# The gates of a recurrent mixer, two heads on a diagonal or one head to each half of the array's rows

## The chip, the cores and the metric

The kernel runs on one core of one Trainium2 chip. The metric is the device time of one launch in microseconds (us). The kernel before took 1994.26 us, the median of three runs (1993.06 to 1998.03).

## The reference, cut to what matters

One decoder layer over 2048 positions (and 16 learned ones ahead of them) of width 1024. After a norm, one projection feeds three token mixers (pooling, a convolution of 31 taps, and a gated linear recurrence), whose outputs are projected back; a squared-ReLU MLP and a last norm follow. The change is in the recurrent mixer, which has 512 channels in 8 heads of 64:

```python
def _rglru_branch(gate_in, x_in, conv_w, conv_b, w_a, b_a, w_x, b_x, lam):
    xc = _causal_depthwise_conv(x_in, conv_w, conv_b)
    xh = xc.reshape(B_, T, RG_HEADS, RG_HD)
    r = jax.nn.sigmoid((jnp.einsum('bthc,hcd->bthd', xh, w_a).reshape(B_, T, D_RNN) + b_a).astype(f32))
    i = jax.nn.sigmoid((jnp.einsum('bthc,hcd->bthd', xh, w_x).reshape(B_, T, D_RNN) + b_x).astype(f32))
    log_a = -RG_C * r * jax.nn.softplus(-lam.astype(f32))
    a = jnp.exp(log_a)
    mult = jnp.sqrt(-jnp.expm1(2.0 * log_a))
    h = _linear_scan(a, mult * (i * xc.astype(f32)))
    return (jax.nn.gelu(gate_in.astype(f32)) * h).astype(x_in.dtype)
```

Each head of 64 channels is multiplied by its own 64 x 64 matrix twice: by w_a for the gate r and by w_x for the gate i.

## The kernel before, in words

Channels lie on the 128 partitions, positions along the free dimension. The sequence is worked through in four chunks of 512 positions; chunk 0 has the 16 learned positions ahead, 528 in all, and is multiplied in two sub-ranges of 264 (`subs_of`, L364).

Every fp32 product is made of three matmuls: each operand is split into a high part (rounded, on ScalarE, L110) and a low part (the rest, on VectorE, L111), and high x high, high x low and low x high are added up in PSUM (`PRODS`, L270). The large weights come from HBM in tiles of 128 x 512 on SyncE's queue, six loaded ahead (WR) and four split ahead (WH); these splits are given a raised priority (`Weights.split`, L257).

The list `items` (L890) is the order of the large products: W, the input projection (`mm_tile`, L278); O, the output projection (`mm_tile`); U, the up-projection (`up_unit`, `mm_block`, L302, seven products of 256 columns in place of eight); D, the down-projection (`mm_tile` and `mm_pair`, L278 and L292). While TensorE works on these, the mixers, norms and loads of the next stage are generators; after each item `pump` (L866) takes steps from them up to a budget. A `Mix` (L647) has a lane for the taps of each half of the convolution and one for the recurrent calls, the pooling and the GELU gates. The framework then orders each engine's instructions by their place in the program and by when their operands are ready; every engine runs its list in that order.

The recurrent mixer is `gen_rg` (L561), called for i = 0 to 3 in every chunk, 16 calls. One call has two heads, head 2i on partitions 0 to 63 and head 2i + 1 on 64 to 127. It computes the short convolution (L566, L568), splits the result (`split_new`), and multiplies it by the gate weights: for each of the two gates a 128 x 128 block with the two heads' matrices on its diagonal and zeros elsewhere (`_blockdiag`, L1023). Each product is three matmuls by `mm3` (L311 to L313) into a PSUM tile of the pool pb, which has two buffers, and a sigmoid on ScalarE (L579) writes r or g with the bias of the channel. After that come an exponential, a tanh and a square root on ScalarE (L584, L586, L589), products on VectorE (L587 to L596) and the scan (L598). The last calls of a chunk come ahead of the output projection of the chunk, which needs all the mixers' outputs (`need_mix`, L883).

The gate weights, 128 x 1024, are loaded and split once by `load_consts` (L207), in two halves of 512 columns, each through one of the two buffers of xr. The weights that `gen_fold` (L156) multiplies ahead of time (pools, pws, w_fold) come through the same two buffers, behind them. The biases lie in one small tensor, `vecs`, a column for 128 channels (`_VECS`, `vc`).

Of the kernel before, what the change touches and what calls it, by code (L numbers as in the profile page):

```python
# [26 lines left out]
F32R = mybir.dt.float32r  # L27
AF = mybir.ActivationFunctionType
ALU = mybir.AluOpType

P = 128
D = 1024
KB = D // P
# [4 lines left out]
FG = 4  # L38
# [19 lines left out]


_VECS = [  # L60
    ("g1", 8), ("g2", 8), ("gf", 8), ("psc", 2), ("lam", 4), ("ba", 4), ("bx", 4),
    ("rcb", 4), ("cb", 2), ("lng", 2), ("lnb", 2), ("rcw", 16), ("cw", 62),
]
_VOFF = {}
# [15 lines left out]
def build(nc, tc, x0, xr, w_in, w_out, w_fold, w_up, w_down, vecs, gates, pools, pws, out):  # L80
# [18 lines left out]
    def t_(tag, cols, bufs, dt=F32):  # L99
        shape = [P] + (list(cols) if isinstance(cols, (list, tuple)) else [cols])  # L100
        return sb.tile(shape, dt, name=nm(tag), tag=tag, bufs=bufs)
# [4 lines left out]
    def ps_back():  # L106
        return pb.tile([P, NT], F32, name=nm("pb"), tag="pb")

    def split(hi, lo, src):
        A.activation(out=hi, in_=src, func=AF.Copy)  # L110
        V.tensor_tensor(out=lo, in0=src, in1=hi.bitcast(F32), op=ALU.subtract)  # L111
# [5 lines left out]
    def vc(name, i=0):  # L117
        o, _ = _VOFF[name]
        return vec[:, o + i : o + i + 1]
# [18 lines left out]
    def w_raw(src, tag="xr", bufs=2):  # L138
        n = src.shape[-1]
        t = t_(tag, 512, bufs)[:, :n]  # L140
        nc.sync.dma_start(out=t, in_=src)
        return t
# [62 lines left out]
        yield 1400  # L205

    def load_consts():  # L207
        hl = t_("c_gw", (2, 1024), 1, F32R)
        for c0 in (0, 512):
            split(hl[:, 0, c0 : c0 + 512], hl[:, 1, c0 : c0 + 512], w_raw(gates[:, c0 : c0 + 512]))  # L210
        cst["gw"] = hl
        yield 1500

        lam = vr("lam")
        s = t_("sp", (8, 4), 1)
        al, e, den, w, w2, q, m = (s[:, i, :] for i in range(7))
        V.tensor_scalar(out=al, in0=lam, scalar1=-1.0, scalar2=None, op0=ALU.mult)
        V.tensor_scalar(out=m, in0=al, scalar1=0.0, scalar2=None, op0=ALU.max)
        V.tensor_tensor(out=al, in0=al, in1=lam, op=ALU.max)
        A.activation(out=e, in_=al, func=AF.Exp, scale=-1.0)  # L220
        V.tensor_scalar(out=den, in0=e, scalar1=2.0, scalar2=None, op0=ALU.add)
        V.reciprocal(den, den)
        V.tensor_tensor(out=w, in0=e, in1=den, op=ALU.mult)
        V.tensor_tensor(out=w2, in0=w, in1=w, op=ALU.mult)
        NTERM = 10
        V.tensor_scalar(out=q, in0=w2, scalar1=1.0 / (2 * NTERM + 1), scalar2=1.0 / (2 * NTERM - 1), op0=ALU.mult, op1=ALU.add)
        for i in range(NTERM - 2, -1, -1):
            V.tensor_tensor(out=q, in0=q, in1=w2, op=ALU.mult)
            V.tensor_scalar(out=q, in0=q, scalar1=1.0 / (2 * i + 1), scalar2=None, op0=ALU.add)
        V.tensor_tensor(out=q, in0=q, in1=w, op=ALU.mult)  # L230
        V.scalar_tensor_tensor(out=q, in0=q, scalar=2.0, in1=m, op0=ALU.mult, op1=ALU.add)
        csp = t_("csp", (2, 4), 1)
        V.tensor_scalar(out=csp[:, 0, :], in0=q, scalar1=-8.0, scalar2=None, op0=ALU.mult)
        V.tensor_scalar(out=csp[:, 1, :], in0=q, scalar1=4.0, scalar2=None, op0=ALU.mult)
        cst["csp"] = csp
        yield 2500
# [127 lines left out]
    def subs_of(o, full=True):  # L364
        if o.c == 0:
            return [(0, 264), (264, 528)] if full else [(META, W0)]
        return [(0, NT)]
# [193 lines left out]
    def gen_rg(o, i):  # L561
# [9 lines left out]
        w = cst["gw"]  # L571
        r = t_("t", W0, TB)
        g = t_("t", W0, TB)
        for q, (dst, bias) in enumerate(((r, "ba"), (g, "bx"))):
            for s0, s1 in subs_of(o):
                ps = ps_back()
                o_ = q * 512 + i * P
                mm3(ps[:, : s1 - s0], [(w[:, 0, o_ : o_ + P], w[:, 1, o_ : o_ + P], hi[:, s0:s1], lo[:, s0:s1])])
                A.activation(out=dst[:, s0:s1], in_=ps[:, : s1 - s0], func=AF.Sigmoid, bias=vc(bias, i))  # L579
        yield 620  # L580
        csp = cst["csp"]
        a = t_("t", W0, TB)
# [450 lines left out]
def _chan(v):  # L1033
    return np.ascontiguousarray(np.reshape(v, (-1, P)).T)


def _layout(inputs):
# [6 lines left out]
    def wt(w):  # L1044
# [6 lines left out]
    cols = {  # L1051
        "g1": _chan(a["mix_norm_g"][0]), "g2": _chan(a["mlp_norm_g"][0]), "gf": _chan(a["final_norm_g"]),
        "psc": _chan(a["pool_scale"][0]), "lam": _chan(a["rg_lambda"][0]), "ba": _chan(a["rg_b_a"][0]),
        "bx": _chan(a["rg_b_x"][0]), "rcb": _chan(a["rg_conv_b"][0]), "cb": _chan(a["convb_dw_b"][0]),
        "lng": _chan(a["convb_ln_g"][0]), "lnb": _chan(a["convb_ln_b"][0]),
        "rcw": rcw.reshape(4, 4, P).transpose(2, 1, 0).reshape(P, 16),
        "cw": cw.reshape(CONVK, 2, P).transpose(2, 1, 0).reshape(P, 2 * CONVK),
    }
    vecs = np.concatenate([cols[n] for n, _ in _VECS], axis=1)
    gates = np.concatenate([_blockdiag(a["rg_w_a"][0]), _blockdiag(a["rg_w_x"][0])], axis=1).reshape(P, 1024)  # L1060
    pools = _blockdiag(a["pool_w"][0].transpose(0, 2, 1)).reshape(P, 256)
    pws = a["convb_pw_w"][0].T.reshape(2, P, 256).transpose(1, 0, 2).reshape(P, 512)
    w_out = a["w_out"][0]
# [6 lines left out]

_SHAPES = {
    "x0": (KB, P, W0), "xr": (NCH - 1, KB, P, NT), "w_in": (14, P, D), "w_out": (KB, P, 512), "w_fold": (4, P, D), "w_up": (32, P, D),
    "w_down": (FG, KB, P, D), "vecs": (P, NVEC), "gates": (P, 1024), "pools": (P, 256), "pws": (P, 512),
}


# [15 lines left out]
```

## Time and profile before

| | |
|---|---|
| runs before, median (lowest, highest) | 1994.26 us (1993.06, 1998.03) |
| the profiled execution's own time | 1989.49 us |
| its span, first to last instruction | 1987.7 us |
| granted TensorE clock, mean | 0.992 |
| TensorE busy, share of the span | 1927.7 us, 97% |
| TensorE weight loads | 1685.3 us, 85% |
| VectorE busy | 1580.9 us, 80% |
| ScalarE busy | 1127.3 us, 57% |
| HBM over the span | 149 GB/s |

In the profile PE is TensorE's matmuls, PEld its weight loads, DVE VectorE, ACT ScalarE, SPq the queue of SyncE, which issues the loads. L579 is line 579 of the kernel. A row of the timeline has the start in us, the duration, engine, line, operation, the tile written and the one read, the shapes and a count; in brackets stands how long the engine was idle ahead of it and what ended that. A row of a tile or line gives the count and the shortest, median and longest duration in ns. The chain is the work that ended last, followed back from the last instruction: each piece was released by the one ahead of it. Matmuls are pipelined: a record is longer than the step to the next one.

### The profile page before, as it was taken

What the parts mean: (1) busy time and instruction counts of PE and PEld (TensorE: products, weight loads), DVE (VectorE), ACT (ScalarE), POOL (GpSimd) and SP (SyncE); (2) the same over time, 40 slices, a digit from 0 to 9 for tenths busy, and PEclk for the clock granted to TensorE, in tenths of its full rate; (3) what the DMA queues carried; (4) which work ended last, traced back from release to release, by engine and by line L of the source; (5) the groups of instructions that cost most, each with busy time, mean ns of one, the idle gap of its engine ahead of it and who ended that gap; (6) DMA issues with size and microseconds to landing.
All of it is one profiled execution on the core that took longest, in us unless ns stands there. A gap on an engine that the chain in (4) does not pass through costs nothing.

```text
span 1987.7 us, 31314 instructions
## 1 busy us (share of the span) xinstructions
PE 1927.7 (97%) x11220; PEld 1685.3 (85%) x11220; DVE 1580.9 (80%) x2557; ACT 1127.3 (57%) x1907; POOL 0.2 (0%) x4
## 2 busy tenths in 40 slices
PE   8999999999999899999999999999999999999997
PEld 7888787888887689898988878988989889889897
DVE  7988787998979899984777689987668587656477
ACT  6575463636586445683666453675648446355364
POOL 0000000000000000000000000000000000000000
PEclk9999999999999999999999999999999999999999
DMA  6415578748443534353534543534445435545354
GB/s 196 133 53 189 181 254 267 254 124 270 125 130 90 186 100 147 110 161 94 165 113 142 172 135 93 163 106 149 132 127 151 135 102 158 162 143 149 112 175 144
DMA packets 166956, 297.77 MB, mean 150 GB/s; under 512 B 18320, under 2 KB 24592, under 8 KB 166800
## 3 DMA queue, kind: packets, MB, share of 16 engines
q1 hardware_dynamic: 166800, 295.77, 48.6%
q8 instruction: 88, 1.44, 0.3%
q14 instruction: 68, 0.56, 0.1%
HBM read 268.43 MB, written 27.26 MB: 149 GB/s over the span
## 4 chain that ended last, share of the span: by engine, by line
PE 73%; DVE 13%; DMA 5%; issue 4%; ACT 4%; SPq 0%; DVEq 0%; ACTq 0%
PE pm L278 41%; PE pm L302 13%; PE pw L302 11%; PE pm L292 7%; DVE wh L111 3%; DMA xr<-d_xr 2%; DMA s<-d_w_up 1%; DVE ca L534 1%; DVE fr L795 1%; ACT wh L110 1%; DVE t L568 1%; PE pb L311 1%; DVE H L111 0%; DVE h L828 0%; DVE U L804 0%
## 5 line engine op out<-in xcount | busy, mean ns | idle before, releaser
L110 ACT ACTIVATE wh<-wr 128x512 fp32r<-128x512 f32 x876 | 546.0, 627 | 669.7 <-PE pm L278 411.5
L278 PE MATMUL pm<-U,wh 128*128 128x512 f32 (+1 forms) x3504 | 790.2, 384 | 1.4 <-DVE wh L111 1.3
L278 PEld LDWEIGHTS pm<-U,wh 128*128 128x128 f32 x3504 | 634.7, 188 | 143.3 <-DVE wh L111 3.1
L111 DVE TENSOR_TENSOR wh<-wr,wh 128x512 fp32r<-128x512 f32 x876 | 598.5, 687 | 187.2 <-ACT wh L110 181.2
L302 PE MATMUL pm<-H,wh 128*128 128x256 f32 x3072 | 392.7, 283 | 4.7 <-DVE wh L111 2.9
L302 PEld LDWEIGHTS pm<-H,wh 128*128 128x128 f32 x3072 | 378.4, 189 | 9.2 <-DVE wh L111 4.4
L302 PE MATMUL pw<-H,wh 128*128 128x256 f32 x2304 | 301.4, 284 | 16.5 <-DVE fr L795 9.2
L302 PEld LDWEIGHTS pw<-H,wh 128*128 128x128 f32 x2304 | 284.9, 190 | 22.3 <-issue 7.2
L278 PE MATMUL pm<-H,wh 128*128 128x512 f32 (+1 forms) x1344 | 272.9, 361 | 13.5 <-ACT H L390 7.3
L278 PEld LDWEIGHTS pm<-H,wh 128*128 128x128 f32 x1344 | 227.7, 193 | 55.7 <-ACT H L390 7.3
L292 PE MATMUL pm<-U,wh 128*128 128x512 f32 (+1 forms) x768 | 176.5, 388 | 0.0
L292 PEld LDWEIGHTS pm<-U,wh 128*128 128x128 f32 x768 | 140.0, 188 | 30.9
L534 DVE SCALAR_TENSOR_TENSOR ca<-Pbv,vec,ca 128x512 f32<-128x512 f32 x180 | 127.0, 745 | 0.0
L828 DVE TENSOR_TENSOR h<-h,pm 128x512 f32<-128x512 f32 (+1 forms) x106 | 71.2, 674 | 49.7 <-PE pm L278 35.9
L804 DVE TENSOR_TENSOR U<-fr,U 128x512 fp32r<-128x512 f32 x128 | 87.3, 685 | 7.9 <-ACT fr L803 7.8
L801 ACT ACTIVATE fr<-fr 128x512 f32<-128x512 f32 x128 | 79.2, 621 | 25.2 <-DVE fr L820 22.5
L795 DVE TENSOR_TENSOR fr<-pw,fr 128x512 f32<-128x512 f32 x128 | 87.8, 686 | 5.5 <-PE pw L302 3.1
L802 ACT ACTIVATE U<-fr 128x512 fp32r<-128x512 f32 x128 | 79.3, 623 | 1.5
L803 ACT ACTIVATE fr<-fr 128x512 f32<-128x512 f32 x128 | 78.7, 618 | 0.3
L346 DVE TENSOR_TENSOR ss<-ss,fr 128x512 f32<-128x512 f32 (+1 forms) x84 | 54.0, 643 | 19.3 <-ACT fr L345 18.2
L337 DVE RECIPROCAL rs<-rs 128x512 f32<-128x512 f32 (+2 forms) x17 | 53.9, 3168 | 10.6 <-ACT rs L335 10.5
L795 DVE TENSOR_TENSOR fr<-pm,q 128x512 f32<-128x512 f32 x64 | 43.7, 683 | 2.8 <-PE pm L302 2.4
(202 smaller groups left out, 1136.3 us busy)
## 6 DMA issues: line engine op xcount, KB each, us to landing
wr<-d_w_down SPq DMA_DIRECT2D x272, 256.0 KB, 3.0
wr<-sums SPq DMA_DIRECT2D x256, 256.0 KB, 3.3
wr<-d_w_up SPq DMA_DIRECT2D x192, 256.0 KB, 3.0
wr<-d_w_in SPq DMA_DIRECT2D x92, 256.0 KB, 2.9
xr<-d_xr SPq DMA_DIRECT2D x56, 256.0 KB, 3.0
t<-d_w_up SPq DMA_DIRECT2D x32, 256.0 KB, 4.0
wr<-wo_fold SPq DMA_DIRECT2D x32, 256.0 KB, 2.7
wr<-d_w_out SPq DMA_DIRECT2D x32, 256.0 KB, 2.7
```

Of the source, the lines that this page charges most:

```text
L110: A.activation(out=hi, in_=src, func=AF.Copy)
L111: V.tensor_tensor(out=lo, in0=src, in1=hi.bitcast(F32), op=ALU.subtract)
L278: T.matmul(ps[:, : s1 - s0], w[k // 4][:, a, (k % 4) * P : (k % 4 + 1) * P], rhs[k][:, b, s0:s1], start=(k == 0 and j == 0), stop=(k == KB ...
L292: T.matmul(ps[:, : s1 - s0], w[k // 4][:, a, (k % 4) * P : (k % 4 + 1) * P], rhs[k][:, b, s0:s1], start=(k == 0 and j == 0), stop=(k == KB ...
L302: T.matmul(ps, w[:, a, k * P : (k + 1) * P], op[k // 2][:, b, (k % 2) * 256 : (k % 2) * 256 + 256], start=(k == 0 and j == 0), stop=(k == ...
L534: V.scalar_tensor_tensor(out=a, in0=o.ub[i][:, k : k + NT], scalar=vc("cw", i * CONVK + k), in1=a, op0=ALU.mult, op1=ALU.add)
L795: V.tensor_tensor(out=out.rearrange("p (a c) -> p a c", a=2), in0=ps.rearrange("p (a c) -> p a c", a=2), in1=x.unsqueeze(1).broadcast_to([ ...
L801: A.activation(out=r, in_=r, func=AF.Relu)
L802: A.activation(out=f[:, 0], in_=r, func=AF.Square)
L803: A.activation(out=r, in_=r, func=AF.Square)
L804: V.tensor_tensor(out=f[:, 1], in0=r, in1=f[:, 0].bitcast(F32), op=ALU.subtract)
L828: V.tensor_tensor(out=h, in0=h, in1=ps[:, : s1 - s0], op=ALU.add)
```

## The change

The block-diagonal gate weights go. The weight tile has 512 columns in place of 1024: for each call i 128 columns, in which rows 0 to 63 hold [w_a | w_x] of head 2i and rows 64 to 127 hold [w_x | w_a] of head 2i + 1. A matmul uses 64 rows, one head, and gives both gates of that head on the 128 partitions of its result: for the even head r on partitions 0 to 63 and i on 64 to 127 (PSUM tile pa), for the odd head i on 0 to 63 and r on 64 to 127 (pb_). The matmuls of the two heads alternate, each head with its own PSUM tile. Six matmuls for each sub-range stay six. The sigmoids are four in place of two for a sub-range, each of 64 partitions: r of both heads stays on its partitions; i is written to the other half of the partitions, so that it comes to lie with its channel. For that the bias of i is stored with its halves exchanged (`bxs`). `load_consts` has one load and one split in place of two.

```diff
-    ("g1", 8), ("g2", 8), ("gf", 8), ("psc", 2), ("lam", 4), ("ba", 4), ("bx", 4),
+    ("g1", 8), ("g2", 8), ("gf", 8), ("psc", 2), ("lam", 4), ("ba", 4), ("bxs", 4),
...
     def load_consts():
-        hl = t_("c_gw", (2, 1024), 1, F32R)
-        for c0 in (0, 512):
-            split(hl[:, 0, c0 : c0 + 512], hl[:, 1, c0 : c0 + 512], w_raw(gates[:, c0 : c0 + 512]))
+        hl = t_("c_gw", (2, 512), 1, F32R)
+        split(hl[:, 0], hl[:, 1], w_raw(gates))
         cst["gw"] = hl
         yield 1500
...
         r = t_("t", W0, TB)
         g = t_("t", W0, TB)
-        for q, (dst, bias) in enumerate(((r, "ba"), (g, "bx"))):
-            for s0, s1 in subs_of(o):
-                ps = ps_back()
-                o_ = q * 512 + i * P
-                mm3(ps[:, : s1 - s0], [(w[:, 0, o_ : o_ + P], w[:, 1, o_ : o_ + P], hi[:, s0:s1], lo[:, s0:s1])])
-                A.activation(out=dst[:, s0:s1], in_=ps[:, : s1 - s0], func=AF.Sigmoid, bias=vc(bias, i))
+
+        low, high = slice(0, 64), slice(64, P)
+        for s0, s1 in subs_of(o):
+            n = s1 - s0
+            pa, pb_ = ps_back(), ps_back()
+            for j, (a, b) in enumerate(PRODS):
+                for ps, h in ((pa, low), (pb_, high)):
+                    T.matmul(ps[:, :n], w[h, a, i * P : (i + 1) * P], (hi, lo)[b][h, s0:s1], start=(j == 0), stop=(j == 2))
+            for dst, ps, to, of, bias in (
+                (r, pa, low, low, "ba"), (r, pb_, high, high, "ba"), (g, pa, low, high, "bxs"), (g, pb_, high, low, "bxs"),
+            ):
+                A.activation(out=dst[to, s0:s1], in_=ps[of, :n], func=AF.Sigmoid, bias=vc(bias, i)[of])
         yield 620
...
-        "bx": _chan(a["rg_b_x"][0]), "rcb": _chan(a["rg_conv_b"][0]), "cb": _chan(a["convb_dw_b"][0]),
+        "bxs": np.roll(_chan(a["rg_b_x"][0]), 64, axis=0), "rcb": _chan(a["rg_conv_b"][0]), "cb": _chan(a["convb_dw_b"][0]),
...
-    gates = np.concatenate([_blockdiag(a["rg_w_a"][0]), _blockdiag(a["rg_w_x"][0])], axis=1).reshape(P, 1024)
+    gates = np.concatenate([
+        np.concatenate([a["rg_w_a"][0][0::2], a["rg_w_x"][0][0::2]], axis=2),
+        np.concatenate([a["rg_w_x"][0][1::2], a["rg_w_a"][0][1::2]], axis=2),
+    ], axis=1).transpose(1, 0, 2).reshape(P, 512)
```

More of the change, by code (lines that the diff above doesn't have):

```diff
@@ L1072 @@
     "x0": (KB, P, W0), "xr": (NCH - 1, KB, P, NT), "w_in": (14, P, D), "w_out": (KB, P, 512), "w_fold": (4, P, D), "w_up": (32, P, D),
-    "w_down": (FG, KB, P, D), "vecs": (P, NVEC), "gates": (P, 1024), "pools": (P, 256), "pws": (P, 512),
+    "w_down": (FG, KB, P, D), "vecs": (P, NVEC), "gates": (P, 512), "pools": (P, 256), "pws": (P, 512),
 }
```

## The prediction

> **What bounds the kernel now.** I read the page first, then the waits, then the gate matmuls by their tile and in the timeline, then the chain of waits in the stretches where they stand.
>
> ```profile
> PE 1927.7 (97%) x11220; PEld 1685.3 (85%) x11220; DVE 1580.9 (80%) x2557; ACT 1127.3 (57%) x1907; POOL 0.2 (0%) x4
> PE 73%; DVE 13%; DMA 5%; issue 4%; ACT 4%; SPq 0%; DVEq 0%; ACTq 0%
> ...
> ACT wh L110 <- PE pm L278: 411.5, 231, 3.2
> ```
>
> TensorE is busy 97% and holds 73% of the chain that ended last; ScalarE mostly waits for TensorE (411.5 us ahead of the weight split of L110). So TensorE time saved is time saved, except where the chain leaves TensorE. The gates are a small part of TensorE's work:
>
> ```profile
> L311 PE MATMUL pb<-hl,c_gw x40: 279/392/498, 81.2 to 1492.1; 128*128 128x512 f32 x24, 128*128 128x264 f32 x16
> L579 ACT ACTIVATE t<-pb,vec x40: 463/678/691, 82.7 to 1495.4; 128x512 f32<-128x512 f32 x24, 128x264 f32<-128x264 f32 x16
> ...
> 568.19 0.41 PE L311 MATMUL pb<-hl,c_gw 128*128 128x512 f32 x1
> ...
> 569.60 1.08 PE L292 MATMUL pm<-U,wh 128*128 128x512 f32 x4
> ```
>
> L311 has 24 + 16 matmuls, and L312 and L313 follow each of them: 72 of 512 columns (12 calls of the recurrent mixer, six each) and 48 of 264 (4 calls in chunk 0, two sub-ranges each). From 568.19 to 569.60 six of 512 columns take 1.41 us, 0.235 us each from start to start; a record of 512 columns lasts 0.39 us (the median of L311), of which 0.16 us are a tail that the next one covers. With 0.12 us for 264 columns (below), all gate matmuls are 72 x 0.235 + 48 x 0.12 = 23 us, and half of that is the most that the change could save.
>
> Where does the chain leave TensorE near the gates? In chunk 0 it runs on VectorE from 96 to 133 us, and in chunk 1 through ScalarE, up to the output projection at 626.59 us, where TensorE stands idle for 2.93 us:
>
> ```profile
> 95.98 1.25 DVE h L598
> ...
> 132.80 0.65 ACT hl L110
> ...
> 571.65 0.69 ACT t L579
> ...
> 612.97 0.63 ACT t L579 x2
> ...
> 626.59 7.62 PE L278 MATMUL pm<-H,wh 128*128 128x512 f32 x25 [2.93 <-DVE H L111]
> ```
>
> At the gates of chunks 2 and 3, and at the first of chunk 1, it stays on TensorE.
>
> **The change part by part.**
>
> *The matmuls.* Their number (120), columns and weight width stay; each now uses 64 rows, and two that follow one another use different halves, different weights and different PSUM banks. No row shows a matmul of 64 rows. A pair lies between one pitch (0.235 us, full overlap) and two (0.47 us, none). What the two would still share is the weight load, and its rate is bounded by the narrow matmuls:
>
> ```profile
> 97.89 0.39 PE L312 MATMUL pb<-hl,c_gw 128*128 128x264 f32 x1 [0.30 <-DVE st L600]
> 98.11 0.29 PE L313 MATMUL pb<-hl,c_gw 128*128 128x264 f32 x1
> 98.24 0.28 PE L312 MATMUL pb<-hl,c_gw 128*128 128x264 f32 x1
> 98.36 0.28 PE L313 MATMUL pb<-hl,c_gw 128*128 128x264 f32 x1
> ```
>
> From 98.24 to 98.36 is 0.12 us with a load in it, so a load takes at most that. I take the low end: 0.24 us for a pair at 512 columns, two loads, since the halves share neither rows, nor operands' partitions, nor a bank. At 264 columns two loads are as long as two matmuls were: no gain in chunk 0. [...]
>
> A call of 512 columns then starts its matmuls at 0, 0.12, 0.24 ... 0.60 and frees TensorE at 0.60 + 0.235 = 0.835 us: 0.57 us of 1.41 are saved. Where the lo half of the operand comes late, the six are cut in two:
>
> ```profile
> 580.91 0.73 PE L311 MATMUL pb<-hl,c_gw 128*128 128x512 f32 x2 [1.17 <-ACT hl L110]
> ...
> 585.70 0.50 PE L312 MATMUL pb<-hl,c_gw 128*128 128x512 f32 x1
> ```
>
> Pieces of two and four save 0.115 + 0.345 = 0.46. Of the 12 calls nine lie where TensorE holds the chain: the first of chunk 1 and all of chunks 2 and 3, of which the last of each chunk is cut. That is 7 x 0.57 + 2 x 0.46 = **-4.9 us**. The other three of chunk 1 (568, 580 and 604 us, 1.5 us more) only lengthen the idle time at 626.59.
>
> *Changes between 128 and 64 rows.* Each uncut piece has one on either side; today there are none. The floor is nothing, if the next weights are still loaded ahead. The next price is an uncovered load, as after a wait: 97.89 to 98.11 is 0.22 us where 0.12 follows at 98.24, so 0.10 us. The ceiling adds the tail: 0.16 + 0.10 = 0.26 us. I take 0.10, the only one that the kernel's own restarts show. The nine calls make 11 pieces, 22 changes: **+2.2 us**. Of chunk 0 only the first call (81 to 84 us) is on TensorE's chain; three pieces, 6 changes: **+0.6 us**. [...]
>
> *The sigmoids.* 40 become 80, of 64 partitions each. Half the partitions don't shorten VectorE's work in this trace (0.70 and 0.71 us), and I take the same for ScalarE:
>
> ```profile
> 117.13 0.70 DVE L512 TENSOR_TENSOR s<-s 64x525 f32<-64x525 f32 x1
> ...
> 125.14 0.71 DVE L515 TENSOR_TENSOR s<-s 128x525 f32<-128x525 f32 x1
> ...
> 101.41 1.28 ACT L584 ACT_TABLE_LOAD   x1
> ...
> 104.02 1.28 ACT L579 ACT_TABLE_LOAD   x1
> ```
>
> By the median and the minimum of L579, the long and the short ones, ScalarE gains 24 x 0.68 + 16 x 0.46 = 24 us. Behind the added sigmoids queue the weight splits of L110, on which TensorE depends, and the rest of the mixer. In chunks 2 and 3 ScalarE's waits for TensorE (411.5 us in all) and four weight tiles split ahead hide 1.36 us a call: nothing; without that cover 8 x 1.36 = 11 us. In chunk 1 the chain passes the sigmoids twice (571.65 and 612.97), each time with two more of 0.68: **+2.7 us** at 626.59 (between 0, if half the rows are cheaper or other work makes room, and 4.1, if a third call counts). In chunk 0 a call has four more of 0.46, 1.9 us. Against that the exponential now comes ahead of the last sigmoid (101.41), and its table is changed back for that one (104.02); with all products of a sub-range ready together these 1.28 us may go. VectorE has its convolution taps to fill in. Of 0 to 3 x 1.9 = 5.7 us I take **+1.0 us**.
>
> *The two PSUM buffers* of the gates are held until the third and fourth sigmoid, not the first and second. In chunk 0 the second sub-range waits for that, two sigmoids longer, at most 1.0 us in each of 4 calls. TensorE has projection matmuls to put between, as it has now: nothing.
>
> *The constants.* One load of gate weights and one split go.
>
> ```profile
> 42.61 3.85 DMA xr<-d_gates
> ...
> 50.90 3.27 DMA xr<-d_w_fold
> ...
> 47.87 0.33 SPq L141 DMA_DIRECT2D xr<-d_pools  x1
> ...
> 54.97 0.50 PE L311 MATMUL pb<-hl,H 128*128 128x512 f32 x1 [2.04 <-ACT hl L148]
> ```
>
> The chain itself passes here: both gate loads hold both buffers of xr, so pools waits on SyncE's queue until the first split has freed one (47.87), and w_fold until pools is read (50.90). With one load pools goes out at once, some 4 us earlier. TensorE waits for that w_fold for 2.04 us: **-2.0 us** (between -2.04 and 0). Next late is TensorE itself.
>
> Sum: -4.9 + 2.2 + 0.6 + 2.7 + 1.0 - 2.0 = **-0.4 us**. On the profiled execution's own 1989.5 us that is 1989.1. That execution lies 4.8 us under the median of the runs, 1994.3, which I keep as the base: 1993.9 us. About 0.3%, 6 us, is what a measurement of this kernel can tell from no change.
>
> **The rivals.**
>
> *A drain at every change (slower).* Place: both sides of each piece, on TensorE. Some 28 pieces (12 in chunk 0, where the second sub-range would no longer be cut, 16 elsewhere), 56 changes at 0.26 us, all on the path: +14.6 - 6.4 (the savings of all 12 calls) - 2.0 + 3.7 (sigmoids) = +9.9 us, 2004.2. It ends slower from 0.19 us a change on, where 56 x 0.19 passes 6 + 4.7. For it: the tail of 0.16 us is there to be waited for. Against: in chunk 0 VectorE holds the chain, so most of the changes there would be hidden. [...]
>
> *Changes free, sigmoids hidden (faster).* -4.9 - 2.0 = -6.9 us, with the 1.5 us of chunk 1 -8.4: 1985.9 to 1987.4. For it: TensorE's 97% and ScalarE's 43% of idle time. Against: in chunk 1 the chain passes through the sigmoids.
>
> *The halves don't overlap*, so the change doesn't do what its form suggests: 0 saved, +2.2 + 0.6 + 2.7 + 1.0 - 2.0 = +4.5 us, 1998.8; with the drain, 7.3 for 2.8, +9.0, 2003.3. For it: no row shows two matmuls overlap beyond the tail. Against: the halves share nothing that the trace shows but the weight load.
>
> **How the numbers follow.** Forecast 0.45, all of it no change. Free changes 0.24: faster. Drain 0.20: slower. No overlap 0.11: 0.03 no change, 0.08 slower. So faster 0.24, same 0.48, slower 0.28. The range reaches from the fastest case, 1985, to the drain, 2005; what a rearranged order of the engines' lists adds or takes no row prices, and that is the part left out.
>
> **What would show it.** Overlap: six gate matmuls of 512 columns free TensorE after 0.84 us; without overlap after 1.4 or more. Changes: the steps into and out of a piece are longer than the usual pitch by 0.10 (mine), 0.26 (drain) or 0. Sigmoids: 80 of them, 0.68 us each at 512 columns, and an idle time of 2.9 + 2.7 = 5.6 us or more at the output projection of chunk 1. Constants: no wait at the first fold matmul near 55 us. I am wrong if the wait of the fold stays, if the one at 626.59 doesn't grow, or if TensorE gains new waits for split weights in chunks 2 and 3.

## The result and the profile after

| | before | after |
|---|---|---|
| runs, median (lowest, highest) | 1993.33 us (1991.4, 1998.03), 6 runs | 2000.44 us (1997.3, 2002.48), 6 runs |
| the profiled execution's own time | 1989.49 us | 1999.71 us |
| its span | 1987.7 us | 1997.9 us |

Three of the six runs before are those of the prediction. After over before is 1.0031, 95% interval 1.002 to 1.0043: the change makes the kernel slower by 6.2 us (4.0 to 8.6). The prediction was 1993.9 us, no change. The time lies within its range, near that of the drain rival, and, as the experiments show, not for that rival's reason.

The page of the kernel after, engines, chain and the group of the sigmoids:

```profile
PE 1932.1 (97%) x11220; PEld 1678.3 (84%) x11220; DVE 1579.1 (79%) x2556; ACT 1150.1 (58%) x1943; POOL 0.2 (0%) x4
...
PE 71%; DVE 12%; ACT 6%; DMA 5%; issue 5%; SPq 0%; DVEq 0%; ACTq 0%
...
L584 ACT ACTIVATE t<-pb,vec 64x512 f32<-64x512 f32 (+1 forms) x80 | 48.1, 601 | 8.6 <-PE pb L580 7.0
```

The matmuls number as many as before. ScalarE's 80 sigmoids take 48.1 us, and its share of the chain goes from 4% to 6% while TensorE's falls from 73% to 71%: the chain spends less of its time on TensorE.

The timeline of TensorE after, at the second to fourth recurrent call of chunk 1 and at the output projection behind them:

```profile
573.43 1.60 PE L301 MATMUL pw<-H,wh 128*128 128x256 f32 x12
574.96 0.97 PE L580 MATMUL pb<-hl,c_gw 64*128 64x512 f32 x6
575.86 1.89 PE L291 MATMUL pm<-U,wh 128*128 128x512 f32 x7
...
595.61 0.49 PE L580 MATMUL pb<-hl,c_gw 64*128 64x512 f32 x2 [2.29 <-ACT hl L110]
596.03 0.96 PE L277 MATMUL pm<-U,wh 128*128 128x512 f32 x3
...
617.02 0.49 PE L580 MATMUL pb<-hl,c_gw 64*128 64x512 f32 x2
617.45 0.73 PE L277 MATMUL pm<-U,wh 128*128 128x512 f32 x2
...
630.03 0.86 PE L277 MATMUL pm<-H,wh 128*128 128x512 f32 x3
631.95 1.23 PE L277 MATMUL pm<-H,wh 128*128 128x512 f32 x3 [1.06 <-ACT wh L110]
636.49 1.22 PE L277 MATMUL pm<-H,wh 128*128 128x512 f32 x2 [3.31 <-ACT H L110]
640.07 10.31 PE L277 MATMUL pm<-H,wh 128*128 128x512 f32 x34 [2.35 <-DVE H L111]
```

Six gate matmuls now free TensorE after 0.90 us (574.96 to 575.86) in place of 1.41: the halves overlap. But the gates of the third call come 20.65 us behind those of the second (595.61), and before it was 12.7 us (568.19 to 580.91). And the 34 matmuls behind the last wait take 10.31 us, 0.30 each, where 41 took 11.32 us before (0.276) and a step at full clock is 0.235:

```profile
626.59 11.32 PE L278 MATMUL pm<-H,wh 128*128 128x512 f32 x41 [2.93 <-DVE H L111]
```

Both belong to a stretch in which the kernel loses time. The windows view of TensorE alone shows it, from the first to the 480th of the same matmuls (the gates' are not counted). Its columns are the stretch, its length, TensorE's busy time (with the matmuls in it), its granted clock, the DMA share and GB/s. Before:

```profile
574.17:707.45 133.28, 120.97 (x493) 0.96 0.40 125
...
626.80:630.21 3.41, 3.41 (x9) 0.51 0.00 0
```

After:

```profile
580.55:718.72 138.17, 123.17 (x493) 0.93 0.39 120
...
634.64:644.88 10.24, 6.04 (x13) 0.50 0.12 36
```

The stretch grows by 4.9 us: idle time (length less busy time) from 12.3 to 15.0, +2.7, and busy time, +2.2, for the same matmuls and those of the gates. The second rows say why they take longer: at the output projection the granted clock is one half for 3.41 us before and for 10.24 us after, and a step from matmul to matmul is 0.43 us there and 0.23 behind it. Over the whole stretch the trace has half the clock for 10.2 us before and 20.5 us after; of that, TensorE is busy in 8.1 and 13.4 us, and half of it, 4.0 and 6.7 us, is lost: 2.65 us more. Of these, 1.3 are lost at the projection; 1.7 in a window of 3.41 us from 597.03 on, behind the wait of 2.29 us at the third call's gates, which before has no counterpart; and 0.3 less than before is lost further on, at the sums of the norm.

The wait of the fold is smaller, not gone (the waits of TensorE after; before it was 2.04 us):

```profile
PE pb L310 <- ACT hl L148: 1.5, 1, 1.5
```

The two profiled executions differ by 10.2 us, more than the medians, and of the rest little can be credited to the change. The first 1200 matmuls, chunk 0's gates among them, take 248.0 us for 245.7 (245.2 to 251.2 in the kernels run here). Between them and this stretch the profiled executions of all kernels run here take between 324 and 335 us (before 328.5, after 332.6) and lose between 2.9 and 9.2 us to the half clock, in no order that goes with the kernels; behind it after is 1.0 us shorter.

### The profile page after: what moved, and what is told of

It is laid out like the page before. It is cut to its first block, busy times and chain, and to the rows that moved or that the text cites. A ratio compares the mean times of both kernels' runs of the same rounds, so it can differ in the third digit from the quotient of the medians.

```text
span 1997.9 us, 31356 instructions
## 1 busy us (share of the span) xinstructions
PE 1932.1 (97%) x11220; PEld 1678.3 (84%) x11220; DVE 1579.1 (79%) x2556; ACT 1150.1 (58%) x1943; POOL 0.2 (0%) x4
## 3 DMA queue, kind: packets, MB, share of 16 engines
q1 hardware_dynamic: 166656, 295.51, 48.1%
## 4 chain that ended last, share of the span: by engine, by line
PE 71%; DVE 12%; ACT 6%; DMA 5%; issue 5%; SPq 0%; DVEq 0%; ACTq 0%
PE pm L277 43%; PE pm L301 10%; PE pw L301 9%; PE pm L291 7%; DVE wh L111 4%; DMA xr<-d_xr 2%; ACT wh L110 2%; DMA s<-d_w_up 1%; DVE fr L800 1%; ACT t L584 1%; DMA sums<-t 1%; DVE ca L533 1%; PE pb L580 1%; DMA wr<-sums 1%; ACT L589 1%
## 5 line engine op out<-in xcount | busy, mean ns | idle before, releaser
L110 ACT ACTIVATE wh<-wr 128x512 fp32r<-128x512 f32 x876 | 545.0, 626 | 650.2 <-PE pm L277 402.2
L584 ACT ACTIVATE t<-pb,vec 64x512 f32<-64x512 f32 (+1 forms) x80 | 48.1, 601 | 8.6 <-PE pb L580 7.0
```

## The experiments

Four theories. **A**: the added sigmoids lengthen the mixers' chain on ScalarE, and the matmuls gain a little. **B**: the change between matmuls of 128 and 64 rows costs more than the overlap gives. **C**: the order in the engines' lists, which the framework makes anew for every program, is what moved. **D**, formed during the work: waits make the granted clock fall, and the matmuls behind them run at half speed. Ratios are to the kernel before on the same chip, with 95% intervals; 0.001 is 2 us.

**Parts of the change.** The half-row matmuls with two whole sigmoids:

```diff
-            for dst, ps, to, of, bias in (
-                (r, pa, low, low, "ba"), (r, pb_, high, high, "ba"), (g, pa, low, high, "bxs"), (g, pb_, high, low, "bxs"),
-            ):
-                A.activation(out=dst[to, s0:s1], in_=ps[of, :n], func=AF.Sigmoid, bias=vc(bias, i)[of])
+            for dst, ps, bias in ((r, pa, "ba"), (g, pb_, "bxs")):
+                A.activation(out=dst[:, s0:s1], in_=ps[:, :n], func=AF.Sigmoid, bias=vc(bias, i))
```

> The kernel after, with two sigmoids of 128 partitions for a sub-range in place of four of 64: r is taken whole from the one PSUM tile and g whole from the other, so half of each gate belongs to the other gate. The matmuls, their order and the single load of the gate weights stay. Theory A (the added sigmoids on ScalarE lengthen the mixer's chain in chunks 0 and 1; the half-row matmuls gain a little): the 7 us of the change go and the gain of the matmuls is left, 1993.3 - 2 to - 5 us, 1988 to 1991. Theory B (the half-row matmuls with their changes of row mode cost the time): still about 2000. Theory C (every edit rearranges the engines' lists and moves the time by several us, in no fixed direction): anywhere from 1987 to 2001.

The diagonal with every sigmoid cut into two of 64 partitions:

```diff
-                A.activation(out=dst[:, s0:s1], in_=ps[:, : s1 - s0], func=AF.Sigmoid, bias=vc(bias, i))
+                for h in (slice(0, 64), slice(64, P)):
+                    A.activation(out=dst[h, s0:s1], in_=ps[h, : s1 - s0], func=AF.Sigmoid, bias=vc(bias, i)[h])
```

> The kernel before, with each of its sigmoids cut into two of 64 partitions, and nothing else: the diagonal matmuls of 128 rows and both loads stay. Theory A: ScalarE has the same 24 us more as in the kernel after, and TensorE gains nothing: 1993.3 + 8 to + 10 us, 2001 to 2003. Theory B: as before, 1993.3 within 2 us. Theory C: anywhere.

The diagonal with one load of gate weights:

```diff
-        for c0 in (0, 512):
+        for c0 in (0,):
...
-                o_ = q * 512 + i * P
+                o_ = i * P
```

> The kernel before, with one load and one split of gate weights in place of two; both gates are multiplied by the first half, so the second gate has the wrong matrix. Matmuls and sigmoids stay as they were. It prices the constants: by the prediction -2.0 us; by theory A, which reads from the trace after that TensorE is no earlier 10 us behind the fold matmul, 0 to -1. Theory C: a shift of several us either way, from an edit that takes away work alone.

The changed form in chunks 2 and 3 only:

```diff
+        if c >= 2:
+            low, high = slice(0, 64), slice(64, P)
...
+        else:
             for q, (dst, bias) in enumerate(((r, "ba"), (g, "bx"))):
```

> The kernel before, with half-row matmuls and four sigmoids in chunks 2 and 3 alone (columns of the diagonal weights stand in for the real ones, the bias of i isn't exchanged; so the gates are wrong there, their time is that of the change). Chunks 0 and 1 and both loads are as before. Theory A: in chunks 2 and 3 ScalarE has slack and TensorE gains 0.33 us in each of six calls and loses 0.3 in the two cut ones: -1.4 us, 1992, hardly to be told from before. Theory B: half of the loss, +3 to +4 us. Theory C: several us either way.

Measured: half rows with two sigmoids 1989.62 us, 0.9977 (0.9967 to 0.9987); diagonal with four sigmoids 2000.64 us, 1.0028 (1.0018 to 1.0039); one load 1992.76 us, 0.9991 (0.998 to 1.0002); chunks 2 and 3 only 1995.07 us, 1.0005 (0.9995 to 1.0015). The matmuls of half the rows gain, 4.6 us together with the one load, and four sigmoids lose 5.6 us without any half-row matmul: B falls. In chunks 2 and 3 the changed form makes no difference that can be told.

**Where the sigmoids cost.** The changed kernel with two whole sigmoids in chunk 1 only:

```diff
+            if c == 1:
+                for dst, ps, bias in ((r, pa, "ba"), (g, pb_, "bxs")):
+                    A.activation(out=dst[:, s0:s1], in_=ps[:, :n], func=AF.Sigmoid, bias=vc(bias, i))
+            else:
                 for dst, ps, to, of, bias in (
```

> The kernel after, with two sigmoids of 128 partitions in place of four in chunk 1 alone (half of each gate belongs to the other gate there). It asks where the added sigmoids cost their time. Theory A1 (the lead-up to the output projection of chunk 1, where the chain runs through ScalarE and TensorE waits): most of the 8 to 11 us that all sigmoids are worth in this kernel go, about 5 us, to some 1995. Rival A2 (chunk 0, where four sigmoids a call are added): 2 us at most, 1998 or more. Rival A3 (spread evenly over ScalarE's 24 us): 5.4/24 of 8 to 11, 2 us.

And in chunk 0 only, with `c == 0` in that line:

> The same in chunk 0 alone: two sigmoids for each of the two sub-ranges in place of four. Theory A1: 1 to 2 us of the loss go, 1998.5 to 1999.5. Rival A2: most of it goes, 1993 to 1995. Rival A3: 7.4/24 of 8 to 11, 3 us, 1997.

Measured: 1991.19 us, 0.9986 (0.9974 to 0.9999), and 1995.77 us, 1.0014 (1.0004 to 1.0024). Chunk 1 holds about 9 of the 10.8 us between the changed kernel and its form with two sigmoids everywhere, chunk 0 some 3.4, which its interval hardly tells from nothing. The third wait at chunk 1's output projection goes with chunk 1's sigmoids.

**Without added sigmoids, by copies.** Two whole sigmoids into r and a further tile y, with biases stored to fit, then three copies of 64 partitions; the function is the reference's. On VectorE:

```diff
+            for dst, ps, bias in ((r, pa, "bpa"), (y, pb_, "bpb")):
+                A.activation(out=dst[:, s0:s1], in_=ps[:, :n], func=AF.Sigmoid, bias=vc(bias, i))
+        nc.vector.tensor_copy(g[low, R], r[high, R])
+        nc.vector.tensor_copy(r[high, R], y[high, R])
+        nc.vector.tensor_copy(g[high, R], y[low, R])
```

> The same with the three copies on VectorE. VectorE is 80% busy and gains 16 x 3 copies of about 0.4 us, 20 us. Theory A: where VectorE holds the chain, in chunk 0 and in the lead-up to the projection of chunk 1, the copies cost their time, 1.2 us a call: 1990 + 4 to 8 us, 1994 to 1998; better than the kernel after, not better than before.

On GpSimd (`nc.gpsimd` in these three lines):

> The half-row matmuls with two sigmoids of 128 partitions for a sub-range (biases stacked to match), which give [r | i] of the even head in one tile and [i | r] of the odd head in another; three copies of 64 partitions on GpSimd, which has nothing else to do, then put the halves in their places, and one more tile of SBUF holds the second result. Everything that is computed is that of the kernel after. Theory A: ScalarE is as free as in the kernel with two sigmoids (1989.6 us beside 1994.7), and the copies add their own length, one after another, to a call's chain, which counts in chunk 1 alone: if a copy is about 1 us, 3 to 6 us there, 1990 to 1996. Rival: the copies disturb VectorE, which reads the same memory, or are far slower; then 2000 or more.

On VectorE again, the last two lines exchanged:

> The half-row gates with two sigmoids of 128 partitions and three copies on VectorE, the last two copies exchanged (g of the high half before r of the high half); the whole function is computed. The theory of the added sigmoids (A): the copies' order changes no work, so the time is that of the earlier kernel with copies on VectorE, 0.9959 of the kernel before, 1985 us, within 2.5 us. The theory of the list (C: a rearranged order of work moves the time by several us by itself): anywhere from 1983 to 1995; over 1988 would say that the earlier 1985 was in part luck of the list.

And the kernel before, with three copies on VectorE that change nothing:

```diff
+        V.tensor_copy(g[low, R], g[low, R])
+        V.tensor_copy(r[high, R], r[high, R])
+        V.tensor_copy(g[high, R], g[high, R])
         yield 620
```

> The kernel before, with the diagonal of two heads and its two sigmoids, and three in-place copies of 64 partitions on VectorE after the sigmoids of each piece (0.42 us each, 1.26 us more in the mixers' chain); the function is unchanged. A: the copies lengthen the chain and nothing pays for them, 0 to 5 us slower: 1994.5 to 1999. C: the copies rearrange the list, which is where some 4 us of the earlier kernel's gain came from: 1989 to 1992.

Measured: VectorE 1985.26 us, 0.9959 (0.9946 to 0.9972); GpSimd 1990.68 us, 0.9987 (0.9975 to 1.0); exchanged 1988.34 us, 0.9968 (0.9956 to 0.998). The first of these is faster than both kernels, where A expected it slower than before. But the useless copies alone give 1987.53 us, 0.9967 (0.9956 to 0.9978): more work, no half-row matmul, and as fast. A has nothing to say to that; what these copies do is move other instructions in the lists (at 175 of TensorE's 11220 places in the trace a matmul of another tile stands than before).

**List or work.** One estimate of the planner changed, and no work:

```diff
-        yield 620
+        yield 900
         csp = cst["csp"]
```

> The kernel before with one estimate of the planner changed (the cost that the recurrent mixer gives back after its gates, 900 in place of 620), so that no work is added or removed and only the order of the engines' lists differs. A: within 2 us of the kernel before, 1992 to 1996. C: a move of 3 us or more either way (ratio under 0.9985 or over 1.0015), which is then the scatter that every comparison between rearranged kernels carries.

Three useless copies of one column in the kernel before:

```diff
+        V.tensor_copy(g[low, 0:1], g[low, 0:1])
+        V.tensor_copy(r[high, 0:1], r[high, 0:1])
+        V.tensor_copy(g[high, 0:1], g[high, 0:1])
         yield 620
```

> The kernel before with three copies on VectorE for each piece, of 64 partitions by one column, in place of copies of the whole width (which gave 0.9967 of the kernel before). The function is unchanged and hardly any work is added. C: the copies gained by rearranging the lists, so this one moves too, by 2 us or more, to either side. A, with a real cause in the copies' time (a VectorE that comes later at something): 1994 within 1.5 us.

A second sigmoid of one column behind each whole one, in the kernel before (the line for the half-row kernel with two sigmoids has `dst[high, s0 : s0 + 1]`, `ps[high, :1]` and `vc(bias, i)[high]`):

```diff
                 A.activation(out=dst[:, s0:s1], in_=ps[:, : s1 - s0], func=AF.Sigmoid, bias=vc(bias, i))
+                A.activation(out=dst[64:P, s0 : s0 + 1], in_=ps[64:P, :1], func=AF.Sigmoid, bias=vc(bias, i)[64:P])
```

> The kernel before, with 40 more sigmoids behind the 40 that it has, each of 64 partitions by one column, which write a column again that stands there already; the function is unchanged. The lists of the engines are rearranged as by the four sigmoids of 64 partitions (388 of TensorE's 11220 instructions stood elsewhere there), but ScalarE's work hardly grows: about 0.2 us for a small one against 0.68. The theory of the sigmoids' time (A): a quarter of the 6 us of the diagonal kernel with four sigmoids, so 1994 to 1997. The theory of the list (C): the rearranged list was what cost 6 us, so 1999 to 2002, or any other move of over 3 us.

> The half-row gates with two sigmoids of 128 partitions, as in the first experiment (mixed gates, 1989.6 us), with two more of 64 partitions by one column for each sub-range, so that the sigmoids number as many as in the changed kernel (2000.4 us). A: the time of the added sigmoids is what counts, so 1990 to 1993. C: the number and order of the instructions is what counts, so 1997 to 2001.

Measured: estimate 1994.23 us, 1.0004 (0.9994 to 1.0013), which says little, since only 10 of TensorE's places changed (237 with the diagonal's four sigmoids, by the same count; the 388 above is a different one); small copies 1990.64 us, 0.9976 (0.9967 to 0.9986); small sigmoids 2005.19 us, 1.0051 (1.0039 to 1.0063) in the diagonal kernel and 1997.41 us, 1.0023 (1.0014 to 1.0032) in the half-row kernel. C said so, A did not. But the small sigmoids are not as light as I had taken them for. ScalarE's timeline of the half-row kernel with them, at the second call:

```profile
574.71 0.26 ACT L583 ACTIVATE t<-pb,vec 64x1 f32<-64x1 f32 x1
...
577.65 0.72 ACT L588 ACTIVATE t<-t,csp 128x512 f32<-128x512 f32 x1
578.39 1.28 ACT L583 ACT_TABLE_LOAD   x1
579.69 0.26 ACT L583 ACTIVATE t<-pb,vec 64x1 f32<-64x1 f32 x1
579.97 0.72 ACT L590 ACTIVATE t<-t,csp 128x512 f32<-128x512 f32 x1
...
591.36 0.63 ACT L110 ACTIVATE hl<-t 128x512 fp32r<-128x512 f32 x1 [2.68 <-DVE t L567]
```

One of them comes behind the exponential and changes the table back (1.28 us): the pair takes 1.8 us, more than two whole ones of 64 partitions. So these two runs do not tell list from work. What they show is in the last row: ScalarE waits 2.68 us for the third call's taps.

**The order.** In the kernel before these taps stand ahead of the second call's square root. ScalarE before (L566 begins the taps of the third call, the table load belongs to the square root, L110 splits the taps' result for the gates):

```profile
577.04 0.80 ACT L566 ACTIVATE t<-Pcx,vec 128x512 f32<-128x512 f32 x1
577.85 1.28 ACT L589 ACT_TABLE_LOAD   x1
579.15 0.63 ACT L589 ACTIVATE t<-t 128x512 f32<-128x512 f32 x1
579.68 0.61 ACT L110 ACTIVATE wh<-wr 128x512 fp32r<-128x512 f32 x1
580.23 0.63 ACT L110 ACTIVATE hl<-t 128x512 fp32r<-128x512 f32 x1
```

After, they stand behind it:

```profile
580.92 1.38 ACT L584 ACTIVATE t<-pb,vec 64x512 f32<-64x512 f32 x2
...
586.01 1.28 ACT L594 ACT_TABLE_LOAD   x1
587.30 0.63 ACT L594 ACTIVATE t<-t 128x512 f32<-128x512 f32 x1
587.84 0.80 ACT L565 ACTIVATE t<-Pcx,vec 128x512 f32<-128x512 f32 x1
...
594.93 0.63 ACT L110 ACTIVATE hl<-t 128x512 fp32r<-128x512 f32 x1 [4.19 <-DVE t L567]
```

VectorE before makes the three taps in one go; after, the first stands among the second call's products and the other two behind its scan (the first row is before, the others after):

```profile
577.87 2.33 DVE L568 SCALAR_TENSOR_TENSOR t<-Pcx,vec,t 128x512 f32<-128x512 f32 x3 [0.63 <-ACT t L566]
...
589.18 0.75 DVE L567 SCALAR_TENSOR_TENSOR t<-Pcx,vec,t 128x512 f32<-128x512 f32 x1
...
591.04 1.28 DVE L603 TENSOR_TENSOR_SCAN Pcx<-t,st,t 128x512 f32<-128x512 f32 x1
...
592.88 0.74 DVE L567 SCALAR_TENSOR_TENSOR t<-Pcx,vec,t 128x512 f32<-128x512 f32 x1
...
594.15 0.75 DVE L567 SCALAR_TENSOR_TENSOR t<-Pcx,vec,t 128x512 f32<-128x512 f32 x1
```

So the changed kernel was given back the order, with all its sigmoids, and the kernel before was given the other one:

```diff
+        with tc.high_priority(EARLY if (c, i) == (1, 2) else 0):
             A.activation(out=xc[:, R], in_=u[:, 0:tw], func=AF.Identity, scale=vc("rcw", i * 4), bias=vc("rcb", i))
...
+            with tc.high_priority(EARLY if (c, i) == (1, 2) else 0):
                 V.scalar_tensor_tensor(out=xc[:, R], in0=u[:, k : k + tw], scalar=vc("rcw", i * 4 + k), in1=xc[:, R], op0=ALU.mult, op1=ALU.add)
```

> The changed kernel with all its four sigmoids; only the taps of the third mixer call of chunk 1 (its scale and bias on ScalarE, its three steps on VectorE) are given the priority that the weight splits have, so that the lists put them ahead of the second call's tanh and square root, as the kernel before has them ahead of the square root. The theory of the order in the lists (C, now with its place: in the kernels with added sigmoids these taps stand behind the second call's square root and scan, and ScalarE waits 2.4 to 4.2 us for them): the wait of 4.2 us goes, the gates of the third call follow those of the second after about 14 us in place of 20.6, and the time is 1994 to 1997, ratio 1.0000 to 1.0017. The theory of the sigmoids' time (A): still 2000, ratio 1.0025 to 1.0038.

```diff
         xc = t_("t", W0, TB)
+        if (c, i) == (1, 2):
+            A.activation(out=xc[:, 0:1], in_=o.late[:, 0:1], func=AF.Copy)
...
         A.activation(out=s[:, R], in_=s[:, R], func=AF.Copy, scale=-1.0, bias=1.0)
+        o.late = s
```

> The kernel before, gates, matmuls and sigmoids as they are; one more ScalarE instruction of one column makes the taps of the third mixer call of chunk 1 depend on the second call's last step on ScalarE before its scan, so that the lists have them behind the square root, as the kernels with added sigmoids do. The function is unchanged. C: ScalarE waits 2 to 4 us for these taps, the gates of the third call come 20 us after those of the second in place of 12.7, and the time is 1998 to 2003, ratio 1.002 to 1.0045. A: one small instruction more, 1994 within 1.5 us.

Measured: order given back 1995.59 us, 1.0004 (0.9991 to 1.0017); order taken away 1994.3 us, 1.0001 (0.9988 to 1.0014). ScalarE in the first of the two no longer waits for the taps:

```profile
583.37 0.80 ACT L566 ACTIVATE t<-Pcx,vec 128x512 f32<-128x512 f32 x1
584.08 0.71 ACT L593 ACTIVATE t<-t,csp 128x512 f32<-128x512 f32 x1
...
588.19 0.61 ACT L110 ACTIVATE hl<-t 128x512 fp32r<-128x512 f32 x1
```

In the second it waits 2.37 us, as C said, and yet the time stays:

```profile
590.36 0.63 ACT L110 ACTIVATE hl<-t 128x512 fp32r<-128x512 f32 x1 [2.37 <-DVE t L570]
```

So the first run goes as C expected and the second as A did: neither holds alone. One length tells the slower kernels from the rest, from the second call's gates to the fourth's in chunk 1 (start to start, each from the profiled execution; for the kernel after 574.96 to 617.02, 42.1 us):

| kernel | ScalarE's wait for the third call's taps, us | second to fourth call, us | ratio |
|---|---|---|---|
| half rows, copies on VectorE | 0 | 35.3 | 0.9959 |
| diagonal, useless copies | 0 | 36.1 | 0.9967 |
| half rows, copies exchanged | 0 | 35.7 | 0.9968 |
| diagonal, small copies | 0 | 36.1 | 0.9976 |
| half rows, two sigmoids | 0 | 36.4 | 0.9977 |
| two sigmoids in chunk 1 | 0 | 36.4 | 0.9986 |
| half rows, copies on GpSimd | 0 | 35.7 | 0.9987 |
| diagonal, one load | 0 | 36.5 | 0.9991 |
| before | 0 | 36.5 | 1 |
| half rows, not alternating (below) | 0 | 36.2 | 1.0000 |
| diagonal, taps behind | 2.4 | 38.9 | 1.0001 |
| diagonal, estimate changed | 0 | 36.5 | 1.0004 |
| after, taps ahead | 0 | 39.1 | 1.0004 |
| half rows in chunks 2 and 3 | 0 | 36.5 | 1.0005 |
| after, waits filled (below) | 4.2 | 42.0 | 1.0013 |
| two sigmoids in chunk 0 | 4.2 | 40.6 | 1.0014 |
| half rows, small sigmoids | 2.7 | 41.2 | 1.0023 |
| diagonal, four sigmoids | 3.9 | 42.0 | 1.0028 |
| after | 4.2 | 42.1 | 1.0031 |
| diagonal, small sigmoids | 2.4 | 42.9 | 1.0051 |

All six kernels over 40 us are slower than before by more than their intervals, none of the others is. Below 40 us the length tells nothing: ratios there go from 0.9959 to 1.0005. The sigmoids alone add 2.6 us (39.1 for 36.5), which is two of 0.68 us in each of two calls, 2.7; the order alone adds 2.4 (38.9); both add 5.6. The order's 2.4 us alone are not lost, and TensorE's waits between 565 and 700 us show how, before:

```profile
PE pb L327 <- ACT hl L110: 6.0, 1, 6.0
PE pm L278 <- DVE H L111: 2.9, 1, 2.9
...
PE pm L278 <- ACT H L110: 0.7, 1, 0.7
```

And in the diagonal kernel with the taps behind:

```profile
PE pb L327 <- ACT hl L110: 4.1, 1, 4.1
PE pm L278 <- ACT H L110: 2.8, 1, 2.8
PE pm L278 <- DVE H L111: 2.6, 1, 2.6
```

The two waits at the projection (H) grow by 1.8 us, and the one behind them, for the column sums of the norm (hl), shrinks by 1.9: one wait pays for the other. With four sigmoids it shrinks no further (4.4 us after, 3.8 with the taps ahead), so what goes beyond seems to be lost.

**The clock.** The changed kernel with matmuls of the first block of chunk 1's output projection done over again, 21 ahead of the wait of 3.31 us and 10 ahead of the last one (that block comes out too large):

```diff
-            for j, (a, b) in enumerate(PRODS):
+            for j, (a, b) in enumerate(again.get(k, PRODS)):
...
-            evac_o(o, j, mm_tile(w, o.u, [full])[0])
+            evac_o(o, j, mm_tile(w, o.u, [full], {0: PRODS * 8, 1: PRODS[:1] * 11 + PRODS[1:]} if (c, j) == (1, 0) else {})[0])
```

> The changed kernel, with 31 matmuls of chunk 1's first block of the output projection done over again where TensorE stands idle ahead of it (21 ahead of the wait of 3.3 us, 10 ahead of the wait of 2.4), so that block is too large by these products; up to there the order on TensorE is the same. The theory of the clock (D: the idle windows halve the granted clock, and the matmuls that follow run at 0.43 us in place of 0.23): the clock stays at 1.00 from 634 to 645 us, the 10 steps of 0.43 us vanish, and the kernel is 1 to 3 us faster than the changed one though it does 7 us more of matmuls: ratio 1.0016 to 1.0026. Without such a clock (A alone): the waits are filled, nothing is won, 2000.4 to 2002 us, ratio 1.0031 to 1.004.

Measured: 1995.37 us, 1.0013 (1.0005 to 1.0022). TensorE's timeline there:

```profile
626.03 9.52 PE L277 MATMUL pm<-H,wh 128*128 128x512 f32 x39
636.09 8.14 PE L277 MATMUL pm<-H,wh 128*128 128x512 f32 x34 [0.53 <-DVE H L111]
```

With the waits filled 34 matmuls take 8.14 us, 0.24 each, in place of 10.31: 2.2 us, the work of the clock alone. 31 matmuls more, some 7 us of work, and the kernel is faster than the changed one, by a little more than D expected; what D says of the clock holds. By the medians it gains 5 us, by the ratios 3.6 (some 1 to 6 by their intervals), by this row 2.2 less 0.8 that the waits for the norm's sums take back (4.4 to 5.2 us), and the whole stretch is 137.6 us long for 138.2. The runs' scatter may hold the rest, and it stays open.

**Overlap.** Half rows and two sigmoids, the low half's three matmuls first, then the high half's:

```diff
-            for j, (a, b) in enumerate(PRODS):
-                for ps, h in ((pa, low), (pb_, high)):
+            for ps, h in ((pa, low), (pb_, high)):
+                for j, (a, b) in enumerate(PRODS):
```

> The half-row gates with two sigmoids of 128 partitions that give mixed gates (as in the first experiment, 0.9977 of the kernel before, 1989.6 us), with the three matmuls of the low half first and then the three of the high half, in place of low and high in turn. If the halves overlap only when neighbours in the list lie in different halves, two of three pairs lose their overlap: about 2 x 0.2 us for each piece, 5 us over the calls on TensorE's chain, so 1994 to 1996. If the engine finds the overlap anyway: 1989.6 within 2.5 us.

Measured: 1994.52 us, 1.0000 (0.999 to 1.001), as the case without overlap said, and yet its trace shows the overlap in full, 0.91 us to the next group:

```profile
579.35 0.98 PE L580 MATMUL pb<-hl,c_gw 64*128 64x512 f32 x6
580.26 1.19 PE L291 MATMUL pm<-U,wh 128*128 128x512 f32 x4
```

So the 5 us between it and the first experiment are not the matmuls'. At 144 of TensorE's places a matmul of another tile stands, and this is the plainest measure of what a rearranged list does outside the length of the table. Why the useless copies gain 6 us is open in the same way; in the profiled executions they gain 4.1 us ahead of the stretch above (324.4 for 328.5), where all kernels scatter.

## Why the prediction was wrong

**The step that failed is the term of the sigmoids**, "+2.7" at 626.59: with "+1.0" in chunk 0 the sum had 3.7 us for them, and in the half-row kernel they cost 10.8. Its mechanism was right: in chunk 1 the chain passes the sigmoids twice, each time with two more of 0.68 us, and they alone do lengthen it by 2.6 us. Chunk 1's sigmoids hold most of the cost, some 9 us; chunk 0's 3.4 us are hardly told from the 1.0 of the sum. Two things were missing behind the term.

First, the lists. The prediction left unpriced "what a rearranged order of the engines' lists adds or takes". With the longer sigmoids the framework put the third call's taps behind the second call's square root and scan: 3.0 us more in the chain (42.1 for 39.1). Of the 10.8 us that the four sigmoids cost the half-row kernel (1.0031 against 0.9977), giving back the order saves half (1.0004); the other half, 5.4 us, stays with the sigmoids, where 3.7 were in the sum. Each half is known to within some 3 us, and useless copies moved the time by more than either, so the times alone don't show this split; the lengths in the traces, 36.5, 39.1 and 42.1 us, speak for it. The order alone, without the sigmoids, loses nothing that can be told (1.0001).

Second, the price of a wait. The sum put a wait at its length: 2.7 us longer, and the idle time of the stretch did grow by 2.7 us (12.3 to 15.0). But the granted clock halves behind two groups of waits, that of 2.29 us at the third call's gates and those of 1.06, 3.31 and 2.35 us at the projection, and over the stretch the matmuls lose another 2.65 us. How much a wait costs this way is not fixed by its length. The kernel with the taps ahead has the same waits at the projection (1.39, 3.31 and 2.35 us) and 10.24 us at half clock there, but no such window at the third call's gates; its stretch is 135.5 us long, and its time is not told from before's. The kernel with two sigmoids in chunk 0 stands idle for 2.29 us there (580 to 590 us) and loses no window either: its clock is 1.00 from 570 to 620 us. In the traces before and after, all stretches at half clock but the last of each are 3.41 us long or two or three times that; by windows of 10 us some of the other kernels have one of about 13.7, four times. Behind a wait of 2.93 us stood one such length (626.85 to 630.26 before), behind one of 2.29 us another (597.03 to 600.44 after); which waits bring one on, these traces don't tell.

**The matmuls.** Predicted -4.9, changes +2.2 and +0.6, constants -2.0: -4.1 together. The half-row kernel with two sigmoids, which has just these, measured -4.6 (-2.6 to -6.6). The size agrees, in part by luck: useless copies moved the time as much, and the parts are not as they were put. The 0.84 us of a call measured 0.90. The cut calls of chunks 2 and 3 are cut into one and five already before (1013.70 and 1014.49 us), not two and four, which by the prediction's own steps saves the same 0.46. "At 264 columns two loads are as long as two matmuls were: no gain" is wrong: there too a pair takes 0.12 us, both loads in it; it is hidden, since chunk 0 is not TensorE's. The prediction set the two matmuls of a pair 0.12 us apart; in the trace after the single records of a pair start 0 to 8 ns apart, mostly 3 to 7. Three such pairs at the pitch of 0.235 us would free TensorE after about 0.71 us and not 0.835, an estimate from these two numbers; over nine calls that is over 1 us. The 0.90 measured has longer steps in it as well.

**The changes.** Each longer step costs 0.10 us, as predicted, but four steps of a piece are longer and not two: into it, its first pair, out of it, and the matmul behind. In the first experiment the single records give 0.213 for 0.116, 0.344 for 0.231, 0.327 for 0.231 and 0.335 for 0.235 us (in the trace after 0.213, 0.340, 0.324 and 0.335). So a piece pays 0.41 us, twice the 0.20 of the sum and below the 0.52 of the drain. An uncut call saves about 0.3 us net, and a cut one, with twice the changes and its first matmul alone, loses as much: for the nine calls 7 x 0.3 - 2 x 0.3 = 1.5 us saved, where the sum had 2.7. The rival of the drain lies nearer to the measured time than the forecast does, 2004.2 and 2000.4, and is wrong: four sigmoids without a single change of rows lose as much.

**The constants.** The wait at the fold was to go, -2.0; it fell from 2.04 to 1.5 us, so one of the prediction's own signs of being wrong, that this wait stays, came for the most part. One load in the diagonal kernel gave 0.9991 (0.998 to 1.0002), 1.8 us that the interval does not tell from nothing.

**Chunks 2 and 3.** "Nothing" for the sigmoids there stands: the changed form in those two chunks alone is 1.0005 (0.9995 to 1.0015).

**Of what would show it:** overlap after 0.84 us (0.90 measured), 80 sigmoids, and over 5.6 us of idle time at chunk 1's projection (1.06, 3.31 and 2.35, 6.7) all came, and each spoke for the forecast while the time did not. The test that would have caught it was not among them: the step from one call's gates to the next.

## What to carry to other kernels

Where a stage hangs on a chain across engines, price a change by the time between two fixed points of that chain in both traces, since the framework may answer a longer instruction with another order, and that can cost as much as the instruction. Count a wait of TensorE of 2 to 3 us with what may follow on the clock: here 3.41 us at half of it behind one of 2.93 us and one of 2.29, 10.24 us at three close together (1.06, 3.31 and 2.35), and none at another of 2.29. Work put into such waits was free here: with 31 matmuls more in them the ratio was 1.0013 for 1.0031. And before a gain of a few us is credited to an edit, add something of the same number of instructions that does nothing: here that alone gave 0.9967.

## What the runs showed of the hardware that I had not expected

The halves of the rows look as if they were taken from the list as from two: with three matmuls of the low half ahead of three of the high half, the first of the high half starts 10 ns after the first of the low half (579.353 and 579.363 in the single records) and ahead of the second of the low half (579.696). That the list has them in this order is read from the program; the trace shows the starts alone.

A sigmoid of 64 partitions by 512 takes 0.68 us, as one of 128 does, and one of 64 by 1 still 0.26 us. A table load takes 1.28 us, and behind 108 of the 121 in the traces before and after the next activation starts within 0.02 us of its end.

A copy of 64 x 512 from one half of the partitions to the other takes 0.42 us on VectorE and about 0.83 us on GpSimd (39.6 us for all 48, chunk 0's of 528 columns among them).
